# Prompt attention: the offsets of both kv groups of a token tile worked out together

## The chip, the cores and the metric

The kernel runs on one core of one Trainium2 chip. The metric is device time in microseconds (us) of one execution of the whole program; 1792.57 us is the median of three timed runs. The program has five compute engines that run their own instruction queues side by side: TensorE (in the profile PE for its matmuls and PEld for its weight loads), VectorE (DVE), ScalarE (ACT), GpSimd (POOL) and SyncE (SP), the last of which here only starts DMA transfers.

## The reference

One step of a hybrid decoder layer: 1024 prompt tokens and 8 sample tokens (one new token each, with 1024 cached tokens behind it) go through RMS norm, one input projection, native sparse attention (NSA) beside a gated DeltaNet (GDN), one output projection and a SwiGLU feed-forward block. The change touches only the attention of the prompt, which is, per token, head and branch:

```
p_cmp = masked_softmax(q . ck)          # 63 compressed blocks
p_sel = masked_softmax(q . k of the top 16 of 16 blocks)
p_win = masked_softmax(q . kw)          # this token and the 512 before it
out   = gate[0] * p_cmp.cv + gate[1] * p_sel.v + gate[2] * p_win.vw
```

There are 8 heads of 64 values in 2 kv groups of 4 heads. The prompt has 16 blocks of 64 tokens and 16 are selected, so its selected branch is causal attention over everything before the token. Everything is float32; the prompt is `x_prompt` of 1 x 1024 x 1024.

## The kernel before, in words

**Units.** The attention of the prompt is worked in 16 units, a token tile i of 128 tokens and a kv group g of 4 heads, in the order `UNITS = [(i, g) for i in (2,1,0,5,4,3,7,6) for g in range(2)]`, so the two groups of a tile follow each other. A unit goes through five streams.

- *Queries* (`load_queries`, line 990 on): the queries of the unit are fetched, split in a high and a low part, transposed into `qt_a`, and their high half copied into `qo`, whose other rows a GpSimd memset (line 998) has set to zero. Both have three buffers.
- *First pass* (`score_maxima`, line 1014 on): for each branch the scores stand with the 128 tokens on partitions, in a PSUM bank S, of which there are three. Line 1044 multiplies with the high part of the keys, line 1045 with the low part. VectorE takes the negated maximum of a row (line 1049) into `nb`, and ScalarE works out the exponentials with that maximum and adds them up into `sm` (line 1051). A row of over 512 keys is done in two halves. GpSimd memsets (line 1020) fill what a branch leaves empty in `nb` and `sm`.
- *Offsets* (`offset_rows`, line 1056 on): from maximum, sum and gate of each of 3 branches x 4 heads comes one number, the offset -max - ln(sum) + ln(gate), in 18 small VectorE instructions on 128 x 12 values (the logarithm is a polynomial). For i of 4 and more four further instructions join the two halves (lines 1067 to 1072). The high and low parts go to `off`, are transposed on TensorE (line 1105, into a bank S), and VectorE writes them into rows 64 to 112 of `qo` (line 1106).
- *Values* (`values_unit`, line 1111 on): the scores again, now with the keys on partitions, in a bank X (lines 1131 and 1132; the rows of `qo` written by the offsets add the offset to each score), one exponential over 512 values (line 1134, `PF`), a mask for some blocks (line 1137), and the weighted sum of the values in bank O (line 1124).
- *Post* (`write_unit`, line 1151 on): the two halves of O are added, and ScalarE's queue stores the unit in memory (`m_scr`), from where the output projection reads it.

**Order.** The instructions of all streams are written out by `schedule` (line 134). Each stream is a generator; it yields its own estimates of cost and delay in us, or a condition under which it may go on, and `schedule` always takes a stream that is due. The conditions are counters of finished units: Q for queries, A for first passes, F for offsets, C for values, P for posts, W for stores. So

```
yield lambda: "aw" in start and done["Q"] > u and done["F"] >= u - 1
yield lambda: done["A"] > u
yield lambda: done["F"] > u and done["P"] >= u - 0
```

are the conditions of first pass, offsets and values of unit u: a first pass begins once the offsets of the unit before the last are done. A compiler step behind it still moves instructions of an engine by when their operands are expected; tiles with several buffers wait for the reader of the buffer's last content.

**Other work beside it.** Ahead of the attention and in its first part the GDN of the prompt runs. The stream `small_streams` then puts in the work of the samples: their GDN (line 1202 and others) once values of one unit are done (`done["C"] >= 1`), then their attention, for which GpSimd starts 32 indirect DMAs (line 1309) into `gx`, a tile of two buffers that two DMAs of SyncE's queue (`cpx`, `kx`) and a VectorE copy read, then the first two thirds of the output projection (line 1530) as soon as the units they need are stored. The last third (line 1545) comes when all units are stored. The feed-forward block starts behind it.

## Time and profile before

| | |
|---|---|
| median of three timed runs | 1792.57 us (1792.04 to 1793.57) |
| the profiled execution | 1790.07 us |
| its span in the trace | 1788.4 us |
| mean granted clock of TensorE | 0.976 of full speed |
| TensorE matmul, weight loads | 1689.1 us, 1502.5 us busy |
| VectorE, ScalarE, GpSimd | 1123.1 us, 832.6 us, 400.5 us busy |
| prompt attention, first pass to last values | 515.7 to 1034 us of the span |

An engine's busy time is the sum of its instructions; matmuls are pipelined, so a busy TensorE is not one at its peak. The idle time in front of an instruction is put down to what came last of all that it waited for. A granted clock below one is a time in which the chip let TensorE run at the lower of its two speeds (1.2 and 2.4 GHz) for a part. The chain of waits is the sequence of work that ended last, followed back from the end of the program; what stands on it takes time of the whole, what does not stand on it need not.

### The profile page before, as it was taken

What the parts mean: (1) busy time and instruction counts of PE and PEld (TensorE: products, weight loads), DVE (VectorE), ACT (ScalarE), POOL (GpSimd) and SP (SyncE); (2) the same over time, 40 slices, a digit from 0 to 9 for tenths busy, and PEclk for the clock granted to TensorE, in tenths of its full rate; (3) what the DMA queues carried; (4) which work ended last, traced back from release to release, by engine and by line L of the source; (5) the groups of instructions that cost most, each with busy time, mean ns of one, the idle gap of its engine ahead of it and who ended that gap; (6) DMA issues with size and microseconds to landing.
All of it is one profiled execution on the core that took longest, in us unless ns stands there. A gap on an engine that the chain in (4) does not pass through costs nothing.

```text
span 1788.4 us, 32029 instructions
## 1 busy us (share of the span) xinstructions
PE 1689.1 (94%) x11985; PEld 1502.5 (84%) x11985; DVE 1123.1 (63%) x2841; ACT 832.6 (47%) x1986; POOL 400.5 (22%) x405
## 2 busy tenths in 40 slices
PE   7999989989989989989999989999999999999998
PEld 7999989989876465555567769999999999999997
DVE  6458874588468766656754377544444444868786
ACT  5567742222356656646864454433333333633222
POOL 1214330222112221110023453332332334100000
PEclk9999999999989889899999999999999999999999
DMA  7135444665331475552444342233222323533212
GB/s 237 41 103 193 177 157 132 213 214 178 103 103 36 129 211 143 161 158 75 148 117 138 117 134 63 97 102 111 84 84 83 97 82 108 178 126 124 96 59 95
DMA packets 247584, 223.81 MB, mean 125 GB/s; under 512 B 76121, under 2 KB 226145, under 8 KB 245246
## 3 DMA queue, kind: packets, MB, share of 16 engines
q1 hardware_dynamic: 232404, 188.79, 34.2%
q0 software_dynamic: 7152, 22.43, 3.9%
q10 hardware_dynamic: 7874, 10.56, 1.8%
q8 instruction: 94, 1.54, 0.3%
q14 instruction: 60, 0.49, 0.1%
HBM read 149.08 MB, written 60.40 MB: 117 GB/s over the span
## 4 chain that ended last, share of the span: by engine, by line
PE 58%; DVE 4%; DMA 4%; ACT 4%; issue 2%; POOL 1%; SPq 0%; POOLq 0%; ACTq 0%; DVEq 0%
PE X L1763 13%; PE Z L1937 6%; PE V L1763 6%; PE Z L1919 5%; PE O L1124 4%; PE g L1530 4%; PE Y L1763 3%; PE mm L1455 2%; DMA gx<-in_cache_nsa_kv_dram,ix 2%; PE S L1044 2%; PE X L1131 2%; PE S L1045 1%; PE Y L1979 1%; PE X L371 1%; PE X L1132 1%
## 5 line engine op out<-in xcount | busy, mean ns | idle before, releaser
L77 DVE TENSOR_TENSOR q<-q,q 128x256 fp32r<-128x256 f32 (+5 forms) x234 | 139.2, 610 | 50.5 <-ACT q L77 49.0
L77 ACT CAST q<-q 128x256 fp32r<-128x256 f32 (+2 forms) x195 | 90.3, 495 | 129.2 <-DVE q L77 79.2
L1051 ACT ACTIVATE S<-S,nb 128x512 f32<-128x512 f32 (+4 forms) x256 | 119.8, 469 | 47.3 <-DVE nb L1049 39.9
L1049 DVE TENSOR_REDUCE nb<-S 128x1 f32<-128x512 f32 (+4 forms) x154 | 96.2, 636 | 14.7 <-PE S L1045 13.3
L1134 ACT ACTIVATE PF<-X 128x512 f32<-128x512 f32 (+1 forms) x148 | 84.9, 595 | 43.6 <-PE X L1132 38.0
L287 PE MATMUL X<-xh,ch_h 128*128 128x344 f32 x288 | 95.0, 330 | 0.0
L371 PE MATMUL X<-wh,xh 128*128 128x320 f32 (+1 forms) x288 | 93.6, 325 | 0.0
L77 DVE TENSOR_TENSOR q<-q,Y 128x258 f32<-128x258 f32 x40 | 16.9, 424 | 121.4 <-PE Y L1763 85.2
L77 ACT COPY q<-X 128x258 f32<-128x258 f32 x80 | 30.0, 375 | 135.5 <-PE X L1763 135.5
L287 PE MATMUL X<-xl,ch_h 128*128 128x344 f32 x288 | 92.7, 322 | 0.0
L287 PE MATMUL X<-xh,ch_l 128*128 128x344 f32 x288 | 92.7, 323 | 0.0
L371 PE MATMUL X<-wh,xl 128*128 128x320 f32 (+1 forms) x288 | 91.3, 317 | 0.1
L371 PE MATMUL X<-wl,xh 128*128 128x320 f32 (+1 forms) x288 | 91.2, 317 | 0.1
L1722 POOL TENSOR_TENSOR q<-q,q 128x512 f32<-128x512 f32 x40 | 58.8, 1470 | 135.2 <-DVE q L77 107.4
L1497 POOL TENSOR_TENSOR wol<-woraw,woh 128x1024 fp32r<-128x1024 f32 x18 | 43.7, 2434 | 88.5 <-ACT woh L1496 88.5
L1137 DVE TENSOR_TENSOR PF<-PF,keep 128x512 f32<-128x512 f32 (+1 forms) x56 | 40.3, 725 | 30.5 <-ACT PF L1134 30.2
L77 POOL TENSOR_TENSOR q<-q,q 128x258 f32<-128x258 f32 (+1 forms) x44 | 46.5, 1068 | 48.9 <-DVE q L77 48.9
L1124 PE MATMUL O<-PF,vs 128*64 128x512 f32 x144 | 54.5, 647 | 1.5 <-DVE o L1155 1.5
L287 PEld LDWEIGHTS X<-xh,ch_h 128*128 128x128 f32 x288 | 54.9, 191 | 0.2 <-ACT craw L245 0.2
L252 DVE SCALAR_TENSOR_TENSOR cacc<-craw,stt,cacc 128x1024 f32<-128x1024 f32 x36 | 53.1, 1475 | 3.0 <-ACT cacc L250 2.7
L287 PEld LDWEIGHTS X<-xl,ch_h 128*128 128x128 f32 x288 | 54.8, 190 | 0.1
L371 PEld LDWEIGHTS X<-wl,xh 128*128 128x128 f32 x288 | 54.4, 189 | 0.4 <-DVE wl L350 0.4
(758 smaller groups left out, 5582.6 us busy)
## 6 DMA issues: line engine op xcount, KB each, us to landing
q<-in_w_gate_up_dram SPq DMA_DIRECT2D x40, 512.0 KB
woraw<-in_w_out_dram SPq DMA_DIRECT2D x23, 512.0 KB
q<-g_scr SPq DMA_DIRECT2D x22, 516.0 KB
q<-in_w_down_dram SPq DMA_DIRECT2D x22, 512.0 KB
g_scr<-q SPq DMA_DIRECT2D x40, 258.0 KB
k_scr<-pack SPq DMA_DIRECT2D x8, 1280.0 KB
packr<-k_scr SPq DMA_DIRECT2D x8, 1280.0 KB
cpx<-gx SPq DMA_DIRECT2D x64, 128.0 KB
```

The source lines that it names most:

```text
L77: i = op(*args, **kw)
L287: mm(p[:, :CH], lhsT=a[:, k], rhs=b[:, k, CH * c:CH * c + CH], start=k == 0 and j == 0, stop=k == 7 and j == 2)
L371: mm(p[:, :ncol], lhsT=a[:, k, c0:c0 + 128], rhs=b[k][:, :ncol], start=k == 0 and j == 0, stop=k == 7 and j == 2)
L1049: V.tensor_reduce(out=nb[:, y, br, h0:h0 + per], in_=pv, op=OP.max, axis=AX.X, negate=True)
L1051: S.activation(pv[:, h], pv[:, h], AF.Exp, bias=nb[:, y, br, h0 + h:h0 + h + 1], accum_out=sm[:, y, br, h0 + h:h0 + h + 1])
L1124: x = mm(O[64 * (n % 2):64 * (n % 2) + 64], lhsT=v, rhs=pf[:w], start=n < 2, stop=n > last - 2)
L1134: S.activation(pf[:w], p[:w], AF.Exp)
L1530: mm(p[:, :n], lhsT=x[:, k], rhs=y[:, :n], start=i == 0 and j == 0, stop=i == 7 and j == 2)
L1722: plan.setdefault(step, []).append(lambda: eng.tensor_tensor(out, x, y, op=op))
L1763: mm(p, lhsT=w[n][:, x, c], rhs=y[:, k, 258 * q:258 * q + 258], start=new and k == 0 and j == 0, stop=k == nk - 1 and j == 2, skip_group_c ...
L1919: mm(p[:, q], lhsT=w[2 * x + k2][:, y, c], rhs=b[:, k, 258 * q:258 * q + 258], start=k2 == 0 and k == 0 and j == 0, stop=k2 == 1 and k == ...
L1937: mm(p[:, q], lhsT=w[n][:, x, c], rhs=y[:, k, 258 * q:258 * q + 258], start=new and k == 0 and j == 0, stop=k == 1 and j == 2, skip_group_ ...
```

## The change

The offsets are worked out once for the two units of a token tile. `nb` and `sm` become one tile for both groups (128 x 2 x 2 x 3 x 4), allocated by the first; `off` holds both groups; the VectorE instructions have 128 x 24 values where they had 128 x 12 (and 128 x 48 where they had 128 x 24). Two transposes go into one bank S, and two writes follow, one into the `qo` of each unit. The offsets of tile k wait for both first passes (`done["A"] > 2 * k + 1`), and a first pass of tile k may start once the offsets of the tile before the last are done. Queries may be fetched four units ahead of the values, not three, and `qt_a` and `qo` have four buffers. In the changed file lines above 1053 move by two or so, and lines below it by five to seven: 998, 1044, 1045, 1105 and 1106 are now 1000, 1046, 1047, 1111 and 1113, and 1020, 1309, 1530, 1545 are 1022, 1316, 1537, 1552.

```diff
@@ -912,7 +912,7 @@
 
     def attention_queries(start, done):
         for u, (i, g) in enumerate(UNITS):
-            yield lambda: "aq" in start and done["A"] >= u - 1 and done["C"] >= u - 3
+            yield lambda: "aq" in start and done["A"] >= u - 1 and done["C"] >= u - 4
             q = load_queries(start["aq"], g, i)
             yield 0.3, 1.0
             start[u] = q()
@@ -921,15 +921,17 @@
 
     def attention_maxima(start, done):
         for u, (i, g) in enumerate(UNITS):
-            yield lambda: "aw" in start and done["Q"] > u and done["F"] >= u - 1
-            start["n", u] = yield from score_maxima(start["aw"], start["stack", g], start[u], g, i)
+            yield lambda: "aw" in start and done["Q"] > u and done["F"] >= u // 2 * 2 - 2
+            if g == 0:
+                start["n", u // 2] = [start["aw"].tile([128, 2, 2, 3, 4], F32, name=n) for n in ("nb", "sm")]
+            yield from score_maxima(start["stack", g], start[u], g, i, *start["n", u // 2])
             done["A"] += 1
 
     def attention_offsets(start, done):
-        for u, (i, g) in enumerate(UNITS):
-            yield lambda: done["A"] > u
-            yield from offset_rows(start["aw"], *start["n", u], start[u][1], g, i)
-            done["F"] += 1
+        for k in range(len(UNITS) // 2):
+            yield lambda: done["A"] > 2 * k + 1
+            yield from offset_rows(start["aw"], *start["n", k], [start[2 * k + g][1] for g in range(2)], UNITS[2 * k][0])
+            done["F"] += 2
 
     def attention_values(start, done):
         for u, (i, g) in enumerate(UNITS):
@@ -993,8 +995,8 @@
         q2 = aw.tile([128, 4, 2, 64], F32R, name="q2")
         S.mul(q2[:, :, 0], qn, 0.125)
         V.scalar_tensor_tensor(q2[:, :, 1], qn, 0.125, q2[:, :, 0].bitcast(F32), op0=OP.mult, op1=OP.subtract)
-        qt = aw.tile([128, 512], F32R, name="qt_a", bufs=3)
-        qo = aw.tile([128, 512], F32R, name="qo", bufs=3)
+        qt = aw.tile([128, 512], F32R, name="qt_a", bufs=4)
+        qo = aw.tile([128, 512], F32R, name="qo", bufs=4)
         G.memset(qo[64:128].bitcast(F32), 0.0)
 
         def finish():
@@ -1011,11 +1013,11 @@
         w0 = 128 * max(0, i - 4)
         return 128 * (i + 1), w0, 128 * (i + 1) - w0
 
-    def score_maxima(aw, st, q, g, i):
+    def score_maxima(st, q, g, i, nb, sm):
         nk, w0, nw_ = window(i)
         md, mw, mc = maskb[:, 0:128], maskb[:, 128:256], maskb[:, 256 + 64 * i:320 + 64 * i]
         qt, qo = q
-        nb, sm = (aw.tile([128, 2, 3, 4], F32, name=n) for n in ("nb", "sm"))
+        nb, sm = nb[:, :, g], sm[:, :, g]
         for x, v in ((nb, 3e38), (sm, 0.0)):
             G.memset(x[:, 1] if nk <= 512 else x[:, 1, 0], v)
         for br, nm, n, k0 in ((0, "c", 64, 0), (1, "s", nk, 0), (2, "w", nw_, w0)):
@@ -1051,29 +1053,32 @@
                         S.activation(pv[:, h], pv[:, h], AF.Exp, bias=nb[:, y, br, h0 + h:h0 + h + 1],
                                      accum_out=sm[:, y, br, h0 + h:h0 + h + 1])
                     yield 0.43 * per * w / 512.0, 0.3
-        return nb, sm
-
-    def offset_rows(aw, nb, sm, qo, g, i):
+
+    def offset_rows(aw, nb, sm, qos, i):
         yield 0.0, 1.5
-        sh = [128, 12]
-        nb, sms = (x.rearrange("p y b h -> p y (b h)") for x in (nb, sm))
-        off = aw.tile([128, 112], F32R, name="off")
-        G.memset(off[:, 0:64].bitcast(F32), 0.0)
-        ov = off[:, 64:112].rearrange("p (x l) -> p x l", l=4)
+        sh = [128, 24]
+        nb, sms = (x.rearrange("p y g b h -> p y (g b h)") for x in (nb, sm))
+        off = aw.tile([128, 2, 112], F32R, name="off")
+        G.memset(off[:, :, 0:64].bitcast(F32), 0.0)
+        ov = off[:, :, 64:112].rearrange("p g (x l) -> p g x l", l=4)
+
+        def two(x):
+            return x.rearrange("p (g x) -> p g x", g=2)
+
         b, sm = nb[:, 0], sms[:, 0]
         if i >= 4:
             b = aw.tile(sh, F32, name="nbm")
-            d = aw.tile([128, 2, 12], F32, name="nbd")
+            d = aw.tile([128, 2, 24], F32, name="nbd")
             V.tensor_tensor(b, nb[:, 0], nb[:, 1], op=OP.min)
-            V.tensor_tensor(d, b[:, None].to_broadcast([128, 2, 12]), nb, op=OP.subtract)
+            V.tensor_tensor(d, b[:, None].to_broadcast([128, 2, 24]), nb, op=OP.subtract)
             S.activation(d, d, AF.Exp)
             yield 0.0, 0.2
             V.tensor_tensor(sms, sms, d, op=OP.mult)
             V.tensor_tensor(sm, sm, sms[:, 1], op=OP.add)
         elif i == 0:
-            V.tensor_scalar(b[:, 0:4], b[:, 0:4], K[:, GE:GE + 1], None, op0=OP.mult)
-        V.tensor_copy(ov[:, :, 0], b)
-        V.tensor_tensor(ov[:, :, 1], b, ov[:, :, 0].bitcast(F32), op=OP.subtract)
+            V.tensor_scalar(two(b)[:, :, 0:4], two(b)[:, :, 0:4], K[:, GE:GE + 1], None, op0=OP.mult)
+        V.tensor_copy(ov[:, :, :, 0], two(b))
+        V.tensor_tensor(ov[:, :, :, 1], two(b), ov[:, :, :, 0].bitcast(F32), op=OP.subtract)
...
@@ -1094,18 +1099,20 @@
         V.scalar_tensor_tensor(r1, r1, 1.0 / 3, z2, op0=OP.add, op1=OP.mult)
         yield 0.0, 0.2
         V.scalar_tensor_tensor(r1, r1, 1.0, t1, op0=OP.add, op1=OP.mult)
-        V.scalar_tensor_tensor(r1, r1, -2.0, sv['gsc'][:, i, 12 * g:12 * g + 12],
+        V.scalar_tensor_tensor(r1, r1, -2.0, sv['gsc'][:, i],
                                op0=OP.mult, op1=OP.subtract)
         yield 0.0, 0.2
         V.scalar_tensor_tensor(r1, ex, -0.6931471805599453, r1, op0=OP.mult, op1=OP.add)
-        V.tensor_copy(ov[:, :, 2], r1)
-        V.tensor_tensor(ov[:, :, 3], r1, ov[:, :, 2].bitcast(F32), op=OP.subtract)
+        V.tensor_copy(ov[:, :, :, 2], two(r1))
+        V.tensor_tensor(ov[:, :, :, 3], two(r1), ov[:, :, :, 2].bitcast(F32), op=OP.subtract)
         yield 0.0, 0.2
         p = bank("S").bitcast(F32R)
-        tr(p[:112, 0:128], off, identr)
-        V.tensor_tensor(qo[64:112].rearrange("p (h t) -> p h t", h=4),
-                        p[64:112, None, 0:128].bitcast(F32).to_broadcast([48, 4, 128]),
-                        K[64:112, BM:BM + 4, None].to_broadcast([48, 4, 128]), op=OP.mult)
+        for g, qo in enumerate(qos):
+            tr(p[:112, 128 * g:128 * g + 128], off[:, g], identr)
+        for g, qo in enumerate(qos):
+            V.tensor_tensor(qo[64:112].rearrange("p (h t) -> p h t", h=4),
+                            p[64:112, None, 128 * g:128 * g + 128].bitcast(F32).to_broadcast([48, 4, 128]),
+                            K[64:112, BM:BM + 4, None].to_broadcast([48, 4, 128]), op=OP.mult)
         yield 0.1, 1.0
 
     def values_unit(aw, st, q, g, i, keep):
```

(Between its last two pieces stands the polynomial, whose instructions are the same on wider tiles.)

Where the instructions stand now is shown at three places. The first is TensorE's opening of the attention, from the first transposed offsets (`S<-identr,off`) to the first low scores of the values (`X<-qo,kcl`). Before, offsets of the first unit came here, with one and a half first passes above these rows:

```order
L1105 MATMUL S<-identr,off 112x128
L1044 MATMUL S<-kwh,qt_a 128x384
L1045 MATMUL S<-kwl,qo 128x384
L1044 MATMUL S<-kwh,qt_a 128x384
L1045 MATMUL S<-kwl,qo 128x384
L1202 MATMUL g<-sg_S,sg_kz 16x128
L1132 MATMUL X<-qo,kcl 64x512
```

And after, with three first passes above these rows or among them, and matmuls of the samples' GDN (`sg_` names) and of the third unit's queries (`q_6212`) between:

```order
L1233 MATMUL g<-K,sg_vn 128x128 x8
L1111 MATMUL S<-identr,off 112x128 x2
L1046 MATMUL S<-ksh,qt_a 128x256
L1047 MATMUL S<-ksl,qo 128x256
L1046 MATMUL S<-ksh,qt_a 128x256
L1047 MATMUL S<-ksl,qo 128x256
L1005 MATMUL S<-identr,q_6212 128x128 x4
L1139 MATMUL X<-qo,kcl 64x512
```

What moved: the first values stand behind the first passes of a whole tile and about half of the next, and the samples' GDN, which stood behind the first values in part, now stands in front of them.

The second place is GpSimd's queue among the gathers (`gx`). Before:

```order
L1309 DMA gx<-in_cache_nsa_kv_dram,ix 128x1024 x2
L998 MEMSET qo 64x512
L1020 MEMSET nb 128x12
L1020 MEMSET sm 128x12
L1309 DMA gx<-in_cache_nsa_kv_dram,ix 128x1024 x2
L1061 MEMSET off 128x64
L1309 DMA gx<-in_cache_nsa_kv_dram,ix 128x1024 x2
L1020 MEMSET nb 128x12
L1020 MEMSET sm 128x12
L998 MEMSET qo 64x512
L1309 DMA gx<-in_cache_nsa_kv_dram,ix 128x1024 x2
```

And after:

```order
L1022 MEMSET nb 128x12 x2
L1316 DMA gx<-in_cache_nsa_kv_dram,ix 128x1024 x2
L1022 MEMSET sm 128x12 x2
L1316 DMA gx<-in_cache_nsa_kv_dram,ix 128x1024
L1062 MEMSET off 128x2x64
L1316 DMA gx<-in_cache_nsa_kv_dram,ix 128x1024 x6
L1022 MEMSET nb 128x4 x2
L1000 MEMSET qo 64x512
L1022 MEMSET sm 128x4 x2
L1316 DMA gx<-in_cache_nsa_kv_dram,ix 128x1024 x2
L1062 MEMSET off 128x2x64
```

What moved: the memsets of `nb`, `sm` and `off` stand together for two units, and the gathers between them stand in longer rows.

The third place is the end of TensorE's attention, the last weighted values (`O<-PF`) and what stands behind them, down to the last third of the output projection (`mm<-`). Before:

```order
L1131 MATMUL X<-qt_a,kwh 128x512
L1132 MATMUL X<-qo,kwl 128x512
L1124 MATMUL O<-PF,vw 64x512 x5
L1567 MATMUL g<-K,sqo 128x1 x3
L1581 MATMUL Y<-K,rn 128x128 x3
L1545 MATMUL mm<-mh,woh 128x264
```

And after, where the last weighted values stand 24 matmuls of the output projection (line 1537, the former 1530) further up than these:

```order
L1537 MATMUL g<-mh,woh 128x384
L1537 MATMUL g<-ml,woh 128x384
L1537 MATMUL g<-mh,wol 128x384
L1588 MATMUL Y<-K,rn 128x128 x3
L1574 MATMUL g<-K,sqo 128x1 x3
L1588 MATMUL Y<-K,rn 128x128 x3
L1552 MATMUL mm<-mh,woh 128x264 x2
```

What moved: part of the second third of the output projection now stands behind the last values of the attention, where nothing but three small norm sums stood.

## Rows read from the trace of the kernel before

**Rows 1.** The first part of the profile's page: for each engine its busy time in us, the share of the span, and the number of instructions.

```profile
PE 1689.1 (94%) x11985; PEld 1502.5 (84%) x11985; DVE 1123.1 (63%) x2841; ACT 832.6 (47%) x1986; POOL 400.5 (22%) x405
```

**Rows 2.** The table by stretches of the span: from and to, length, busy time of PE, PEld, DVE, ACT and POOL in us (with the number of instructions), the granted clock of TensorE, the busy share of the DMA engines, and GB/s. The first five stretches are the prompt's attention, the last is what follows it.

```profile
510.00:550.00 40.00, 33.62 (x173) 23.68 (x172) 28.47 (x105) 23.34 (x79) 6.89 (x19) 0.83 0.29 81
550.00:604.00 54.00, 52.20 (x281) 32.92 (x280) 45.47 (x153) 35.56 (x125) 8.77 (x22) 0.91 0.23 58
604.00:800.00 196.00, 172.84 (x1044) 110.08 (x1044) 124.05 (x362) 120.03 (x351) 35.74 (x57) 0.94 0.62 174
800.00:930.00 130.00, 122.73 (x731) 76.31 (x728) 86.37 (x245) 95.44 (x273) 9.00 (x15) 0.97 0.33 107
930.00:1034.00 104.00, 99.25 (x474) 73.58 (x473) 40.91 (x60) 44.29 (x72) 44.80 (x22) 0.98 0.42 126
1034.00:1073.00 39.00, 31.82 (x235) 28.98 (x234) 28.36 (x53) 19.92 (x44) 23.43 (x22) 1.00 0.53 143
```

**Rows 3.** The instructions of three lines: the first pass's scores on the compressed keys (its first matmul of each unit), the transposes of the offsets, and the weighted values. After the count: shortest, median and longest duration in ns, then the start of the first and of the last in us.

```profile
L1044 PEld LDWEIGHTS S<-kch,qt_a x64: 186/192/333, 515.7 to 895.9; 128*128 128x128 f32 x64
...
L1105 PE MATMUL S<-identr,off x16: 219/272/356, 542.2 to 927.7; 128*112 128x128 f32 x16
...
L1124 PEld LDWEIGHTS O<-PF,vs x144: 132/136/231, 546.9 to 1026.8; 128*64 128x64 f32 x144
```

**Rows 4.** VectorE's groups by line between 500 and 940 us: out<-in, shapes, count, then busy time in us and mean ns of one, then idle time before them. The lines of the offsets make 25 groups of this list: the write of `qo` (line 1106), and 24 others from the costliest (line 1102) down to line 1072 and, smaller still, the one of the two units with i = 0 (line 1074). Shown are the write, the costliest, and those which tell the two widths 12 and 24 apart.

```profile
L1106 DVE TENSOR_TENSOR qo<-S,K 48x512 fp32r<-48x512 f32 x16 | 11.1, 695 | 8.3 <-PE S L1105 8.0
...
L1102 DVE TENSOR_TENSOR off<-r,off 128x12 fp32r<-128x12 f32 x16 | 3.7, 229 | 0.3
...
L1071 DVE TENSOR_TENSOR sm<-sm,nbd 128x24 f32<-128x24 f32 x8 | 1.4, 181 | 13.6 <-ACT S L1051 11.3 <-ACT nbd L1069 2.3
...
L1068 DVE TENSOR_TENSOR nbd<-nbm,nb 128x24 f32<-128x24 f32 x8 | 1.4, 179 | 0.1
...
L1067 DVE TENSOR_TENSOR nbm<-nb 128x12 f32<-128x12 f32 x8 | 1.4, 169 | 0.3
L1072 DVE TENSOR_TENSOR sm<-sm 128x12 f32<-128x12 f32 x8 | 1.3, 168 | 0.2
```

**Rows 5.** The chain of waits in order of time: start in us, duration in us, what. 82 of its pieces lie on lines 1067 to 1106, 15.3 us together; these are the first and the last of them.

```profile
530.03 0.08 DVE off L1075
...
927.78 0.20 PE S L1105
```

**Rows 6.** The list of waits between 500 and 1040 us: which engine waits at which line, for what, then us in total, how many times, and the longest.

```profile
ACT S L1051 <- DVE nb L1049: 39.9, 43, 4.3
...
PEld S L1044 <- ACT S L1051: 23.1, 34, 1.9
...
PE S L1044 <- ACT S L1051: 6.5, 10, 1.3
```

**Rows 7.** First the instructions of the line of the gathers (columns as in rows 3), with the time from issue to landing of one; then, from the list of waits between 604 and 800 us (columns as in rows 6), GpSimd's memsets.

```profile
L1309 POOL DMA_INDIRECT gx<-in_cache_nsa_kv_dram,ix x32: 933/940/1234, 603.8 to 788.1; - x32
...
DMA to landing us min/median/max: 3.9/4.7/6.5
...
POOL qo L998 <- PE X L1132: 29.5, 5, 13.6
POOL sm L1020 <- DVE t L1087: 23.4, 5, 10.7
...
POOL off L1061 <- PE S L1105: 10.8, 3, 5.4
...
POOL nb L1020 <- ACT S L1051: 7.9, 4, 4.0
...
POOL nb L1020 <- DVE lex L1079: 5.8, 1, 5.8
```

**Rows 8.** The timeline around the last weighted values: start in us, duration, engine, line, what; in brackets the idle time in front of it and what ended that. (ACTq is ScalarE's queue starting a transfer.)

```profile
1025.25 0.33 PE L1530 MATMUL g<-mh,woh 128*128 128x384 f32 x1
...
1025.42 0.33 PE L1530 MATMUL g<-ml,woh 128*128 128x384 f32 x1
...
1033.09 0.19 PEld L1124 LDWEIGHTS O<-PF,vw 128*64 128x64 f32 x2 [2.08 <-DVE PF L1137]
...
1034.20 0.58 ACT L1154 COPY o<-O 64x512 f32<-64x512 f32 x1 [2.75 <-PE O L1124]
...
1035.57 0.68 DVE L1155 TENSOR_TENSOR o<-O,o 64x512 f32<-64x512 f32 x1
...
1036.28 0.58 ACTq L1156 DMA_DIRECT2D m_scr<-o  x1
...
1043.26 0.19 PEld L1545 LDWEIGHTS mm<-ml,woh 128*128 128x128 f32 x1 [1.91 <-DVE ml L153]
```

## The prediction

> **What bounds the kernel now.** I read the page's shares first: TensorE is busy 94% of the span and VectorE 63% [rows 1]. So a faster VectorE pays only where TensorE waits. Next comes the table by stretches [rows 2]. The attention of the prompt runs from about 510 to 1034 us, and the kernel's other stretches hold none of the changed instructions. In those 524 us TensorE is busy 33.62 + 52.20 + 172.84 + 122.73 + 99.25 = 480.6 us, so it is idle for 43.4 us, and 7.2 us more in the 39 us behind it (39 - 31.82). Besides, the granted clock is below one: 0.83, 0.91, 0.94, 0.97, 0.98. A clock of 0.83 over 40 us is 6.8 us of work lost; over the five stretches it is 6.8 + 4.9 + 11.8 + 3.9 + 2.1 = 29.5 us. TensorE's work is the same after the change, matmul for matmul, so all that can be won or lost is part of 43 us of idle time, 30 us of slow clock and 7 us behind the stage.
>
> Where does the change reach that idle time? The chain of waits shows 82 pieces on the lines of the offsets (1067 to 1106), 15.3 us together, between 530 and 928 us [rows 5]. The list of waits shows TensorE's weight loads of the first pass waiting 23.1 us for ScalarE to free a bank S, 34 times, and its matmuls 6.5 us more; ScalarE there waits 39.9 us for VectorE's maxima [rows 6]. GpSimd's list shows its memsets holding up the queue in which the 32 gathers of the samples stand [rows 7].
>
> **The change part by part.**
>
> *Fewer, wider VectorE instructions.* A unit had 19 instructions of offsets, four more in the 8 units with two halves and one more in the 2 units with i = 0: 16 x 19 + 32 + 2 = 338. A pair has 18 and two writes of qo, four more in 4 pairs, one in one: 8 x 20 + 16 + 1 = 177. The write of qo (694 ns) stays at 16 [rows 4]. The others are 24 groups, from 3.7 us down to 1.3 us [rows 4], 59.4 us together, and half of that goes: 29.7 us. They become 24 wide. Rows for both widths stand in the trace: 169 and 168 ns at 12, 179 and 181 ns at 24 [rows 4], 7% more, so 2 us comes back. VectorE loses about 28 us of work. That is no term of the sum; only the next two are.
>
> *The steps on the chain.* 15.3 us of the chain are offset steps [rows 5]. With half as many runs of the same length, 7.7 us leave it at the most, and nothing at the least, if the pass beside them is late next. What is late next is TensorE itself in the stretches where it is 94 to 97% busy, and a bank S in the others. I take -5, two thirds of the way, as the pieces are short and scattered, not one long stall.
>
> *The banks of the first pass.* VectorE works 28.47 + 45.47 + 124.05 + 86.37 + 40.91 = 325 us in the stage [rows 2], and 59 of them are offsets, 18%. If that share of the 29.6 us of bank waits [rows 6] is due to offsets queued ahead of a maximum, it is 5.4 us, and half is 2.7. At the most all of VectorE's relief shows (half of 29.6, 14.8), at the least nothing. I take -2, near the share.
>
> *GpSimd's queue.* Between 604 and 800 us the gathers share it with memsets that wait: sm 23.4, qo 29.5, off 10.8, nb 7.9 and 5.8 us [rows 7], 77 us in all. The 32 gathers start from 603.8 to 788.1 us, 5.9 us apart, and one lands in 4.7 us. The order shows memsets of nb, sm and off in fewer places between the gathers, and the buffers they reset belong to a pair before the last, not to a unit before the last; qo has four buffers for three. So the gathers come sooner, and their transposes too. TensorE is idle for 196 - 172.84 = 23.2 us there. Most of it is not the gathers' alone. A gather's floor, landing and the copies behind it over two buffers, is not far below 5.9 us. I take -3, between 0 and -12 (half the idle time).
>
> *The opening.* The first offsets now need the first pass of both units, so TensorE does the first pass of three units where it did one and a half, before the first weighted values. Before, the first pass starts at 515.7 us, the first offsets are turned at 542.2 and the first values follow at 546.9 [rows 3]; TensorE is idle 6.4 us in 510 to 550 and loses 6.8 us to the clock. The order shows about 20 us of first pass more ahead of the first values. At the rate of that stretch (13.2 us lost in 40) this costs 6.6 us; beside the samples' matmuls that now stand there it may cost nothing. I take +3. From the second pair on, the wait for both units is covered: the values of the pair before are queued beside the first pass of this pair, some 1.4 us of matmul for each block.
>
> *The end.* Before, the last weighted values wait 2.08 us for a mask, TensorE has nothing else, and its output's way through ScalarE, VectorE, memory and back ends with a wait of 1.91 us at 1043.26 [rows 8]. After, 24 matmuls of the output projection stand behind the last values; at 0.17 us from start to start [rows 8] that is 4.1 us of cover. TensorE is idle 7.2 us in 1034 to 1073 [rows 2]. I take -3, between 0 and -7.2.
>
> *The rest.* Eight memsets less on GpSimd, the same transposes, the same DMAs: nothing, since GpSimd is busy 22% of the span [rows 1] and 35.74 of the 196 us with the gathers [rows 2].
>
> Sum: -5 - 2 - 3 + 3 - 3 = -10 us. The profiled execution took 1790.07 us (its span 1788.4 and 1.7 around it), so 1780. The median of the three timed runs is 1792.57, 2.5 above it, so the forecast is 1782.5 us; all times below are on this scale.
>
> **The rivals.**
>
> *A. The relief is hidden.* VectorE is not the bound, the order of TensorE is fixed, and it waits for the next thing instead: the opening's +3 to +6.6 eats the end's -3, and the chain keeps all but a few of its 15.3 us. For it: 34 bank waits of 0.7 us are what three banks cost, with or without offsets. Against it: the offsets are on the chain 82 times. Time 1789 to 1796, say 1792.
>
> *B. The opening decides, and it is slower.* One mechanism: while only first passes run, TensorE goes round the three banks S with short stops, and its clock stays down. In 510 to 550 us it was granted 0.83 of 2.4 GHz, that is, a third of the stretch at 1.2 GHz, with 16% idle [rows 2]. If the 20 us more go at that rate, 6.6 us are lost, and the two following stretches start with the attention behind: the samples' gathers, which wait for the first values before them in the program, start later by as much. Gains of the other terms below 3 us then leave +4 to +10: 1797 to 1803, say 1799. It decides if the first values come later than about 570 us. The Trainium skill, in "TensorE: Matmul & The Clock Gate", section "A second HAM failure mode: psum-queue depth-cycling", says that groups of matmuls cycling through PSUM banks with micro-idles between them make the clock swing between its two levels; by that rule this is the likelier end. The trace agrees with the rule in this stretch: 0.83 here against 1.00 in the 39 us behind the stage, though those have 18% idle.
>
> *C. The gathers were the bound in the middle.* If the freed queue shortens 604 to 800 us by half of its idle time and of its lost clock (23.2 + 11.8, half 17.5, in place of my -3), the sum is -24: 1768. For it: 77 us of waiting memsets in front of gathers [rows 7]. Against it: TensorE did other work for 88% of that time.
>
> *D. It doesn't do what it says.* The instructions are fewer for certain (the order shows it); what could fail is that they run back to back. It falls together with A.
>
> **How the numbers follow.** The forecast's own case (a gain of 4 to 17 us, 1776 to 1789) gets 0.52, C 0.12, A with D 0.20, B 0.16. About 0.2%, 3.6 us, is what a measurement of this kernel can tell from no change: faster means below 1789.0, slower above 1796.2. Faster takes the forecast's case, C and a little of A's lower edge, 0.66; slower takes B without its lower edge, and a little of A's upper one, 0.16; 0.18 is left for no change. The range reaches from the near half of C to the near edge of B, 1770 to 1797.
>
> **What would show it.** Right: VectorE's rows of the offsets at 8 a line and near 180 ns; chain pieces on them near 8 us; bank waits of the first pass below 29 us; the 32 gathers closer than 5.9 us; less than 7.2 us idle in the 39 us behind the last values. Wrong: first values later than 570 us with a clock of 0.83 up to there (B); gathers as far apart as before and a first weighted value as late as before (A). The forecast as a whole is wrong if TensorE's idle time plus lost clock between 510 us and the end of the stage, 73 us now, isn't smaller by 4 us at least.

## The result and the profile after

The changed kernel takes 1810.67 us (median of four runs, 1802.82 to 1814.57) against 1792.3 us for the kernel before on the same chip. The ratio is 1.0101 with a 95% interval of 1.0076 to 1.0125, so the change makes the kernel slower by 18 us. The forecast was 1782.5 us with a range from 1770 to 1797.

The profiled execution is the fastest of the four, 1802.82 us. Its first part of the page and the chain's shares:

```profile
PE 1694.0 (94%) x11985; PEld 1505.7 (84%) x11985; DVE 1106.6 (61%) x2680; ACT 833.8 (46%) x1982; POOL 399.2 (22%) x397
...
PE 55%; DMA 5%; issue 4%; DVE 4%; ACT 4%; POOL 1%; SPq 0%; POOLq 0%; ACTq 0%; DVEq 0%
```

VectorE has 161 instructions and 16.5 us less than in [rows 1], TensorE the same 11985 matmuls. On the chain TensorE has 55% where the page of before has 58%, transfers 5% for 4%, and "issue", time in which an engine waited for nothing that the profile shows, 4% for 2%. These shares are no measure of the loss: up to 516 us the chain now runs along GpSimd's stores of the input projection, with "issue" between them (six pieces of 1.9 to 5.2 us from 490.8 us on), where it ran along TensorE's matmuls.

The table by stretches, to be laid beside [rows 2], and one row each for the whole way from 510 us to the first matmul of the feed-forward block, of after and then, in a fence of its own, of before:

```profile
510.00:550.00 40.00, 30.38 (x174) 22.79 (x172) 21.68 (x69) 18.74 (x61) 12.82 (x25) 0.81 0.34 93
550.00:604.00 54.00, 49.95 (x262) 33.69 (x261) 39.87 (x117) 37.40 (x130) 2.81 (x17) 0.92 0.19 52
604.00:800.00 196.00, 172.68 (x1020) 109.64 (x1020) 118.61 (x319) 118.69 (x352) 36.01 (x55) 0.91 0.58 159
800.00:930.00 130.00, 122.49 (x725) 70.50 (x725) 81.11 (x194) 96.46 (x270) 9.80 (x9) 1.00 0.37 118
930.00:1034.00 104.00, 100.71 (x478) 74.94 (x476) 44.43 (x63) 45.53 (x77) 38.90 (x19) 0.98 0.44 132
1034.00:1073.00 39.00, 31.02 (x189) 26.57 (x187) 21.78 (x41) 15.50 (x28) 16.55 (x12) 0.91 0.50 139
...
510.00:1133.30 623.30, 564.17 (x3304) 394.04 (x3303) 373.84 (x876) 360.05 (x974) 145.19 (x162) 0.95 0.42 123
```

```profile
510.00:1118.90 608.90, 557.32 (x3302) 390.01 (x3301) 389.61 (x1035) 358.13 (x976) 144.21 (x168) 0.95 0.43 125
```

The way to the feed-forward block is 14.4 us longer. TensorE is idle for 59.1 us of it (623.3 - 564.2) where it was 51.6 (608.9 - 557.3). The other 6.9 us are busy time, 564.2 for 557.3 us with the same matmuls. The clock can account for most of that, though over the whole way it is 0.95 in both: counted by stretches as in the prediction, 7.6 + 4.3 + 17.6 + 0 + 2.1 + 3.5 = 35.1 us are lost where it was 29.5 (and nothing in the sixth stretch).

The opening is where it begins. TensorE's timeline of after:

```profile
514.61 0.30 PE L371 MATMUL X<-wh,xl 128*128 128x320 f32 x1
519.97 0.69 PE L1176 MATMUL g<-sg_d,K 8*128 8x64 f32 x2 [5.06 <-DVE sg_d L1174]
520.59 0.69 PE L1185 MATMUL g<-sg_sq,K 128*128 128x64 f32 x2
523.98 0.75 PE L1005 MATMUL S<-identr,q 128*128 128x128 f32 x4 [2.70 <-DVE q L997]
...
525.40 0.42 PE L1046 MATMUL S<-kch,qt_a 128*128 128x64 f32 x1 [0.43 <-ACT qt_a L1006]
```

Behind the last matmul of the input projection (line 371) TensorE stands idle for 5.06 us. Then come two small matmuls of the samples' GDN, then another idle 2.70 us, and only at 523.98 us the transposes of the first queries (line 1005). Before, these followed the projection at once, and the first pass began at 515.7 us [rows 3]; now it begins at 525.40. The line of before:

```profile
514.54 0.46 PE L1003 MATMUL S<-identr,q 128*128 128x128 f32 x4
```

VectorE shows what both waited for:

```profile
518.25 0.48 DVE L393 TENSOR_TENSOR ta<-r,rope 8x320 f32<-8x320 f32 x1 [5.32 <-DMA r<-q]
...
523.50 0.42 DVE L997 SCALAR_TENSOR_TENSOR q<-qn,q 128x256 fp32r<-128x256 f32 x1
```

It waits 5.32 us for a transfer of the samples' own queries (`r<-q`), with the first queries of the prompt (line 997) behind that in its queue. And the queries come late themselves. SyncE's queue of after, then of before:

```profile
514.94 0.37 SPq L1206 DMA_DIRECT2D sg_S<-in_state_gdn_S_dram  x1
515.47 0.86 SPq L994 DMA_DIRECT2D qn<-q_scr  x2
```

```profile
502.74 14.50 SPq L992 DMA_DIRECT2D qn<-q_scr  x5
517.33 5.55 SPq L1199 DMA_DIRECT2D sg_S<-in_state_gdn_S_dram  x8
```

A load of the samples' GDN state (`sg_S`) now stands in front of the first load of queries (`qn`). It waits for the end of the input projection, since its tile lies where the projection's inputs were; the list of waits of SyncE's queue says so:

```profile
SPq L1206 <- PE X L371: 19.3, 1, 19.3
```

So the first queries are fetched at 515.47 us, 12.7 us later than before. The transposes of the offsets and the weighted values, as in [rows 3], and the gathers, as in [rows 7]:

```profile
L1111 PE MATMUL S<-identr,off x16: 225/261/454, 564.4 to 920.1; 128*112 128x128 f32 x16
```

```profile
L1131 PEld LDWEIGHTS O<-PF,vs x144: 132/135/233, 568.2 to 1031.1; 128*64 128x64 f32 x144
```

```profile
L1316 POOL DMA_INDIRECT gx<-in_cache_nsa_kv_dram,ix x32: 932/937/1439, 621.3 to 807.1; - x32
```

First values 21.3 us late, first gather 17.5 us, last gather 19.0 us. The opening by these two points, up to the first values and up to the first gather, of before and then of after:

```profile
510.00:546.90 36.90, 30.52 (x163) 22.63 (x161) 25.85 (x91) 20.47 (x68) 6.68 (x17) 0.81 0.31 84
510.00:603.80 93.80, 85.61 (x452) 56.56 (x451) 73.77 (x257) 58.70 (x203) 15.48 (x40) 0.87 0.26 68
```

```profile
510.00:568.20 58.20, 46.58 (x271) 37.78 (x269) 36.41 (x117) 29.92 (x103) 13.32 (x30) 0.79 0.29 80
510.00:621.30 111.30, 96.05 (x491) 63.64 (x490) 73.63 (x225) 65.48 (x219) 17.34 (x46) 0.89 0.24 65
```

Up to the first gather TensorE is idle for 15.3 us where it was 8.2, so 7.1 of the 7.5 us of new idle time lie in the opening. The lost clock does not: 0.11 x 111.3 and 0.13 x 93.8 are both 12.2 us.

Why should a load change its place in SyncE's queue? The program's list of tiles shows one thing that the diff does not: the fourth buffers of `qt_a` and `qo` make the queries' pool 4096 bytes per partition longer.

```
bytes per partition            before              after
pool of the queries            87776 to 108768     87776 to 112864
  its last buffer of qo        106720 to 108768    110816 to 112864
nat, first of three buffers    111328 to 112736    the same
```

`nat` holds projected rows until they are stored, among them the prompt's queries; in both traces the last of these stores starts at 513 us. The fourth `qo` lies on it. This is theory M: the overlap, and not the pairing, moves the queries behind the samples. Its rival is that the pairing's longer opening does it (theory O). Not only the buffer on `nat` comes late but all that the pool gets first, the mask tile `keep` too (its load starts at 516.5 us, before at 505.6). It goes with its pool the other way as well: in e2 and e9 below `keep` lies in the next pool, which reaches over `nat` in every kernel, and its load starts at 517.4 and 516.4 us. Which rule of the compiler's reordering does that is not seen from here.

### The profile page after: what moved, and what is told of

Same layout as the page of the kernel before. It is cut to its first block, busy times and chain, and to the rows that moved or that the text cites. A ratio compares the mean times of both kernels' runs of the same rounds, so it can differ in the third digit from the quotient of the medians.

```text
span 1801.0 us, 31831 instructions
## 1 busy us (share of the span) xinstructions
PE 1694.0 (94%) x11985; PEld 1505.7 (84%) x11985; DVE 1106.6 (61%) x2680; ACT 833.8 (46%) x1982; POOL 399.2 (22%) x397
## 4 chain that ended last, share of the span: by engine, by line
PE 55%; DMA 5%; issue 4%; DVE 4%; ACT 4%; POOL 1%; SPq 0%; POOLq 0%; ACTq 0%; DVEq 0%
PE X L1770 12%; PE Z L1944 6%; PE V L1770 6%; PE Z L1926 5%; PE O L1131 4%; PE g L1537 3%; PE Y L1770 3%; DMA gx<-in_cache_nsa_kv_dram,ix 3%; PE mm L1462 2%; PE S L1046 2%; ACT S L1053 2%; PE X L1138 2%; PE Y L1986 1%; PE S L1047 1%; PE X L1139 1%
## 5 line engine op out<-in xcount | busy, mean ns | idle before, releaser
L77 ACT CAST q<-q 128x256 fp32r<-128x256 f32 (+2 forms) x195 | 90.3, 494 | 126.2 <-DVE q L77 78.9
L1141 ACT ACTIVATE PF<-X 128x512 f32<-128x512 f32 (+1 forms) x148 | 85.1, 595 | 47.8 <-PE X L1139 45.2
L77 DVE TENSOR_TENSOR q<-q,Y 128x258 f32<-128x258 f32 x40 | 16.9, 424 | 121.0 <-PE Y L1770 87.9
L1144 DVE TENSOR_TENSOR PF<-PF,keep 128x512 f32<-128x512 f32 (+1 forms) x56 | 44.0, 792 | 32.3 <-ACT PF L1141 32.1
L1316 POOL DMA_INDIRECT gx<-in_cache_nsa_kv_dram,ix x32 | 31.3, 979 | 111.9 <-DVE nb L1051 21.0
L371 PEld LDWEIGHTS X<-wh,xl 128*128 128x128 f32 x288 | 55.2, 192 | 0.4 <-DVE xl L153 0.4
```

The costliest lines, as they stand in the source:

```text
L77: i = op(*args, **kw)
L371: mm(p[:, :ncol], lhsT=a[:, k, c0:c0 + 128], rhs=b[k][:, :ncol], start=k == 0 and j == 0, stop=k == 7 and j == 2)
L1141: S.activation(pf[:w], p[:w], AF.Exp)
```

## The experiments

Each ratio is to runs of the kernel before on the same chip: e1 to e4 on one, e5 to e8 on a second, e9 to e12 on a third. Single runs of one kernel differ by up to 13 us here (the kernel before from 1787.5 to 1800.1, e9 from 1788.1 to 1800.9), so the ratios decide and a profile is one draw.

**e1: before, with 4096 unused bytes.**

```diff
+                        pad = aq.tile([128, 1024], F32, name="pad", bufs=1)
+                        V.memset(pad[:, 0:1], 0.0)
```

> The kernel before, with one unused tile of 4096 bytes per partition put into the pool of the queries; nothing else is changed. Theory M (memory): the change's fourth buffers of qt_a and qo make that pool 4096 bytes longer, its end goes from byte 108768 to 112864 and so reaches over the two buffers of nat (from 111328 on), which the last stores of the projected queries still read at 513 us; the first queries then come 12.7 us later, as in the changed kernel (502.74 -> 515.47 us). It expects here the first transposes of the queries at about 524 us and not 514.5, TensorE idle some 5 us in front of them, the first gather about 10 us later than 603.8, and 1798 to 1810 us. Theory O (opening: the wait for the first passes of both units, rival B of the prediction) expects no difference from before: 1790 to 1794 us.

Ratio 1.0069 (1.0047 to 1.0091), median 1806.55 us. The attention's code is as before, and 12 of the 18 us are there. The first gather, at 611.3 us, is 7.5 us late, where about 10 were expected. The same rows of SyncE's queue and of TensorE:

```profile
515.81 0.37 SPq L1201 DMA_DIRECT2D sg_S<-in_state_gdn_S_dram  x1
516.29 0.92 SPq L994 DMA_DIRECT2D qn<-q_scr  x2
```

```profile
521.11 0.69 PE L1171 MATMUL g<-sg_d,K 8*128 8x64 f32 x2 [5.33 <-DVE sg_d L1169]
525.12 0.75 PE L1005 MATMUL S<-identr,q 128*128 128x128 f32 x4 [2.70 <-DVE q L997]
```

The load order of the changed kernel and both its idle times, here 5.33 and 2.70 us, come with 4096 bytes of nothing.

**e8: the same with 2560 bytes**, which end where `nat` begins.

```diff
+                        pad = aq.tile([128, 640], F32, name="pad", bufs=1)
+                        V.memset(pad[:, 0:1], 0.0)
```

> Control of e1: the kernel before with an unused tile of 2560 bytes, so that the queries' pool ends at byte 111328, where nat begins, without reaching over it. Theory M: no difference from before, 1790 to 1795 us, first transposes of the queries at 514 to 517 us. If any shift of the tiles behind it would do what e1 did, it is 1800 us or more.

Ratio 1.0008 (0.9993 to 1.0023). The instructions of all engines stand as before, but for the pad's memset, and the first transposes come at 515.8 us. So it is no shift of tiles that costs; it is reaching over `nat`.

**e2: the change without the overlap.**

```diff
-                        keep = aq.tile([128, CW - KD], BF, name="keep", bufs=1)
+                        keep = aw.tile([128, CW - KD], BF, name="keep", bufs=1)
```

> The changed kernel, with the mask tile keep (2560 bytes) moved from the queries' pool to the next one, so that the queries' pool ends at byte 110304, in front of nat's 111328. All work is the same. Theory M expects the first transposes of the queries back at about 514.5 us, the first values at 552 to 560 us in place of 568.2, the first gather at 603 to 612 us in place of 621.3, and 1786 to 1798 us. Theory O expects the changed kernel's time: 1803 to 1814 us.

Ratio 1.0020 (1.0004 to 1.0035), median 1797.89 us. SyncE's queue has the queries first again, long before the projection ends:

```profile
498.36 20.23 SPq L994 DMA_DIRECT2D qn<-q_scr  x5
518.64 1.53 SPq L1206 DMA_DIRECT2D sg_S<-in_state_gdn_S_dram  x3
```

The first transposes start at 515.7 us and the first values at 560.4, close to what was expected, and the time is at the upper end of its range. The first gather, at 624.1, did not come earlier, against the expectation.

**e12: the changed kernel again**, beside e9 to e11.

> The changed kernel itself, beside the others on one chip. Against e2 it tells what the overlap with nat costs within the change. Theory M: as at first, 1803 to 1814 us, 8 to 15 us more than e2 had over its own before.

Ratio 1.0108 (1.0092 to 1.0123). Against e2 that is 0.88%, 15.8 us, for the overlap alone (uncertain by 0.22%, 4 us; 8 to 15 us were expected).

**e9: the buffers and queries ahead, without the pairing.**

```diff
-            yield lambda: "aq" in start and done["A"] >= u - 1 and done["C"] >= u - 3
+            yield lambda: "aq" in start and done["A"] >= u - 1 and done["C"] >= u - 4
...
-        qt = aw.tile([128, 512], F32R, name="qt_a", bufs=3)
-        qo = aw.tile([128, 512], F32R, name="qo", bufs=3)
+        qt = aw.tile([128, 512], F32R, name="qt_a", bufs=4)
+        qo = aw.tile([128, 512], F32R, name="qo", bufs=4)
```

(and `keep` moved as in e2)

> The kernel before with the fourth buffers of qt_a and qo and the queries up to four units ahead, offsets per unit as before, and keep moved, so that no tile of the queries' pool lies on nat. Together with e3 (the same with the pairing's conditions) it tells what the extra buffers do by themselves. Theory M: without the overlap they are free: 1789 to 1796 us, first gather at 600 to 606 us. If more queries ahead disturb the order of VectorE or ScalarE, 1797 us or more.

Ratio 1.0005 (0.9989 to 1.0021): free to within 4 us, where they overlap nothing. The first gather, at 608.5 us, came later than expected.

**e3: e9 with the pairing's conditions, offsets still narrow.**

```diff
-            yield lambda: "aw" in start and done["Q"] > u and done["F"] >= u - 1
+            yield lambda: "aw" in start and done["Q"] > u and done["F"] >= u // 2 * 2 - 2
...
-            yield lambda: done["A"] > u
+            yield lambda: done["A"] > u // 2 * 2 + 1
```

> As e2 in its buffers and in its conditions (offsets of a tile only when both first passes are done, queries up to four units ahead, keep moved), but with the offsets worked out per unit on 128x12 values as before, one unit after the other. It tells the pairing's order from the wider instructions. If the wider instructions are worth anything (28 us of VectorE's time, the prediction's terms of 5 and 2 us), it is 3 to 8 us slower than e2; if VectorE's relief is hidden (rival A), it is within 2 us of e2.

Ratio 1.0043 (1.0021 to 1.0066). The pairing's conditions, which let the offsets wait for both first passes, cost 0.38% over e9, 7 us (uncertain by 5). The wider instructions (e2 against e3) give 0.23%, 4 us, back, but with these intervals (together 0.27% either way) that is not clear of nothing. So neither "3 to 8 us slower than e2" nor rival A's "within 2 us" is settled by it.

**e4: before, samples started later; e7: before, samples started earlier.**

```diff
-        yield lambda: "free" in start and done["C"] >= 1
+        yield lambda: "free" in start and done["C"] >= 2
```

> The kernel before, with the samples' stream started after the values of two units, not of one. Theory S (the samples' serial stream of GDN, 32 gathers, residual and output projection is what sets the end of the stage): whatever the first gather is late, the end is late by too, some 10 to 15 us: 1800 to 1808 us. Rival: the gathers have slack, TensorE fills the time with the prompt's attention: 1790 to 1795 us.

Ratio 1.0078 (1.0053 to 1.0104), first gather at 632.2 us. As theory S expected. In e7 the condition is `done["A"] >= 1`:

> The kernel before, with the samples' stream started after the first first pass and not after the first values. Counterpart to e4, which started it later (first gather 28 us later, 14 us slower). Theory S: the first gather comes at 590 to 600 us in place of 603.8, and the time is 1784 to 1790 us. If the samples' stream is not what ends last once it is early enough (the prompt's attention is then late next), it stays within 2 us of before.

Ratio 1.0061 (1.0043 to 1.0079), with the first gather 25 us earlier, at 579.0. Theory S falls: the samples' stream is not what the end waits for alone.

**e5: pairs from the second token tile on; e6: e2 with the samples after two first passes; e10: after three.**

```diff
-            yield lambda: done["A"] > 2 * k + 1
-            yield from offset_rows(start["aw"], *start["n", k], [start[2 * k + g][1] for g in range(2)], UNITS[2 * k][0])
-            done["F"] += 2
+            for gs in ((0, 1),) if k else ((0,), (1,)):
+                yield lambda: done["A"] > 2 * k + gs[-1]
...
```

> As e2 (the changed kernel, keep moved, so no overlap with nat), but the offsets of the first token tile are worked out unit by unit; from the second tile on they are worked out for both units together on 128x24 values. TensorE's order then has the first transposed offsets and the first values at their old places in the opening (first values at about 548 us in place of e2's 560.4). Theory S+O (the pairing loses by the late first values, since the samples' stream waits for them): first gather at about 604 us in place of 624.1, and 1786 to 1793 us, 4 to 8 us under e2. Theory P (the pairing loses in every tile, since offsets of two units come as one longer piece in front of the values): no more than 2 us under e2.

Ratio 1.0064 (1.0044 to 1.0084): the first values are back at 547.4 us, but the first gather comes at 616.5, not at 604, and nothing is won. Theory S+O falls. Theory P is met as it was put (not faster than e2), but it does not say why e5 is 0.44% slower than e2. In e6 and e10 the samples' condition of e2 is `done["A"] >= 2` and `done["A"] >= 3`:

> As e2, but the samples' stream starts after two first passes and not after the values of one unit; the pairing is in all tiles. Theory S (the start of the samples' stream sets the end of the stage): first gather 5 to 15 us before e2's 624.1, and 1788 to 1795 us, 3 to 8 us under e2. Theory P: as e2, within 2 us of 1798.

> As e2, but the samples' stream starts after three first passes; e6 started it after two (first gather at 590.6 us, last values 13 us late), e2 after the first values (624.1 us, output projection 9 us late). Theory T (two streams on one TensorE end the stage together: the end comes 85 us behind the last values or 90 us behind the last matmul of the middle part of the output projection, whichever is later): with the first gather between, both are late by less, 1792 to 1798 us. If the pairing itself costs TensorE time wherever the samples stand, 1798 us or more.

Ratios 1.0058 (1.0036 to 1.0080) and 1.0070 (1.0055 to 1.0084), first gathers at 590.6 and 596.0. Theories S and P miss in e6 and theory T in e10, whose other branch, 1798 us or more, is met: earlier samples make the pairing slower.

**e11: pairs in the last two tiles only**, where no gather is left.

```diff
-            for gs in ((0, 1),) if k else ((0,), (1,)):
+            for gs in ((0, 1),) if k >= 6 else ((0,), (1,)):
...
```

> Offsets per unit for the first six token tiles (i = 2, 1, 0, 5, 4, 3), with the conditions of before; together only for the last two (i = 7, 6), behind all gathers. Four buffers, keep moved. Nothing of the samples' stream up to the last gather is disturbed. Theory T expects before's time less what a quarter of the relief is worth: 1789 to 1795 us. A candidate for the best version.

Ratio 1.0032 (1.0019 to 1.0045), 5.7 us slower: a miss, and no better version.

**What the profiles have in common.** One row for each kernel's profiled execution; starts in us of the first values, the first gather, the last weighted values (O), the last matmul of the middle third of the output projection (P) and the feed-forward block's first matmul (F).

| kernel | first values | first gather | O | P | F | F - O | F - P |
|---|---|---|---|---|---|---|---|
| before | 546.9 | 603.8 | 1033.6 | 1028.8 | 1118.9 | **85.3** | **90.1** |
| after | 568.2 | 621.3 | 1039.2 | 1043.8 | 1133.3 | 94.1 | **89.5** |
| e1 | 561.0 | 611.3 | 1040.0 | 1035.2 | 1125.3 | **85.3** | **90.1** |
| e2 | 560.4 | 624.1 | 1033.2 | 1037.8 | 1127.9 | 94.7 | **90.1** |
| e3 | 560.1 | 620.3 | 1032.9 | 1037.5 | 1127.0 | 94.1 | **89.5** |
| e4 | 550.6 | 632.2 | 1036.8 | 1043.5 | 1133.5 | 96.7 | **90.0** |
| e5 | 547.4 | 616.5 | 1033.8 | 1037.4 | 1129.0 | 95.2 | **91.6** |
| e6 | 563.0 | 590.6 | 1046.8 | 1042.0 | 1132.3 | **85.5** | **90.3** |
| e7 | 558.8 | 579.0 | 1044.6 | 1029.6 | 1129.4 | **84.8** | 99.8 |
| e8 | 549.9 | 604.0 | 1036.5 | 1031.7 | 1121.9 | **85.4** | **90.2** |
| e9 | 548.3 | 608.5 | 1042.3 | 1037.4 | 1127.6 | **85.3** | **90.2** |
| e10 | 557.3 | 596.0 | 1044.1 | 1039.3 | 1129.7 | **85.6** | **90.4** |
| e11 | 547.2 | 608.8 | 1034.9 | 1034.2 | 1122.8 | 87.9 | **88.6** |
| e12 | 569.4 | 622.6 | 1046.4 | 1051.0 | 1140.4 | 94.0 | **89.4** |

A single profile scatters: e8 has the instructions of before and e12 those of after, and their F stand 3.0 and 7.1 us later. What holds in all fourteen is the two last columns: the feed-forward block starts some 85 us behind the last values or 90 us behind the projection, whichever is later, to within 1.5 us; from its start to the end of the span it is 667.7 to 670.1 us. The two numbers can be told apart only where one stream is late alone, 84.8 in e7 and 89.4 to 90.1 in after, e2, e3, e4 and e12. By these both bounds bind at the same moment before: 1033.6 + 84.8 = 1118.4, 1028.8 + 90.1 = 1118.9. The two streams share one TensorE, and either one put ahead makes the other late: after, e2, e3, e4, e5 and e12 are late by P, e7 by O, e1, e6, e8, e9 and e10 by both, as before, with P always some 4.8 us in front of O, and e11 stands between. That is theory T. As a forecast of times it failed in e10 and e11. It says which stream is late in each kernel; it does not say why a pair's wait makes the sum of both worse, and no run here does.

## Why the prediction was wrong

*The opening.* This is the step that failed. It was put at +3 us, at most +6.6, for first passes in a stretch of slow clock, with the samples' matmuls as cover, and "the same DMAs" were put at nothing. The order rows showed those matmuls moved forward, and the prediction took them for cover, without asking what they wait for. They wait for a transfer, and so does VectorE. The DMAs are the same, but the first load of queries had moved behind a load on SyncE's queue that must wait for the input projection; that queue's order shows it, and the prediction did not look there, nor had it a term for the fourth buffers that moved it. Measured: 5.06 + 2.70 us of idle TensorE, the first values 21.3 us late where e2, the same change without the overlap, has them 13.5 us late, and 12 us (e1) to 16 us (e12 against e2) at the end.

*The clock.* The prediction looked for it in the opening, where it had no part: 12.2 us lost up to the first gather, as before. Behind it some 5 us more are lost in all: more in 604 to 800 (0.91 for 0.94) and 1034 to 1073 (0.91 for 1.00), less in 800 to 930 (1.00 for 0.97) [rows 2]. No term had that. It is not the draw of one profile alone: e12's five executions have a mean granted clock of 0.970, the 23 of before beside them 0.974, which is, as an estimate, 7 of their 19 us. Whether the new order lowers the clock there or the waits do, no run shows.

*"TensorE's work is the same, so all that can be lost is part of the idle time"* was no bound for the loss: new idle time can be made, and was. The prediction's last sign says so: idle time and lost clock from 510 to 1034 us, 73 us before, are 47.8 + 31.6 = 79 us after.

*Fewer, wider instructions.* Right. All groups of the offsets but the write of `qo` sum to 30.5 us, where they took 59.9 (the 59.4 of the prediction leave out the one for i = 0); 28 us less was forecast. VectorE's busy time as a whole fell by 16.5 us only: part of these short instructions overlap their neighbours in the trace, and the other instructions take 6.3 us more (1069.9 to 1076.2). Three of the rows:

```profile
L1113 DVE TENSOR_TENSOR qo<-S,K 48x512 fp32r<-48x512 f32 x16 | 10.6, 691 | 4.2 <-PE S L1111 4.0
...
L1107 DVE TENSOR_TENSOR off<-r,off 128x24 fp32r<-128x24 f32 x8 | 1.6, 203 | 0.2
L1101 DVE SCALAR_TENSOR_TENSOR r<-r,t 128x24 f32<-128x24 f32 x8 | 1.4, 181 | 0.2
```

*The steps on the chain (-5).* They did leave it: 53 pieces and 10.4 us, where there were 82 and 15.3 [rows 5]. But the way is longer all the same: on the chain between 495 us and the feed-forward block the gathers have 47 us where they had 36. ("Issue" has 45 where it had 28, but 18 of these lie in front of 516 us, beside the input projection.) What leaves a chain is no gain while another wait stands ready.

*The banks (-2).* Nothing came. The waits of [rows 6] after the change:

```profile
ACT S L1053 <- DVE nb L1051: 39.0, 42, 3.6
...
PEld S L1046 <- ACT S L1053: 23.1, 36, 1.6
...
PE S L1046 <- ACT S L1053: 8.2, 17, 0.8
```

39.0, 23.1 and 8.2 us for 39.9, 23.1 and 6.5. Offsets in VectorE's queue were not what held up the maxima; this part of rival A was right.

*GpSimd's queue (-3).* Nothing came, and rival C falls with it. The memsets that waited between the first and the last gather did wait less, 43 us in all, where they had 77 [rows 7]; these are the longest of each tile after the change, in 621 to 808 us:

```profile
POOL nb L1022 <- ACT S L1053: 17.2, 1, 17.2
...
POOL qo L1000 <- PE X L1139: 12.3, 4, 5.4
...
POOL off L1062 <- PE S L1111: 6.9, 1, 6.9
...
POOL sm L1022 <- DVE t L1092: 3.7, 2, 2.3
```

But from the first to the last gather it is 185.8 us, before 184.3, and 182 to 195 in all fourteen kernels: neither waiting memsets nor the pairing set their pace.

*The end (-3).* The cover came: after the last values at 1039.2 us matmuls of the output projection go on to 1043.8. But behind them the norm's small sums now wait uncovered:

```profile
1048.01 0.83 PE L1574 MATMUL g<-K,sqo 128*128 128x1 f32 x6 [3.17 <-DVE sqo L1569]
...
1051.48 1.62 PE L1588 MATMUL Y<-K,rn 128*128 128x128 f32 x6 [2.65 <-DVE rn L1579]
```

The wait moved from the last values to the projection, 3.17 + 2.65 us, since that is now what ends last (P in the table).

*The rivals.* B gave the direction, and first values at 568.2 us are just short of its mark of 570, but that was luck: 15.8 us of the loss are the overlap's, which B does not name, and its price of 4 to 10 us was half of the 18 at the most. Its mechanism, a clock held down by more first passes, is not what made it. Up to the first values the clock is indeed low for longer (0.79 over 58.2 us, 0.81 over 36.9 before), but e1, with no first pass more, has 0.77 over 51.0 us, and up to the first gather no more is lost than before. The rule that B cited from the Trainium skill ("TensorE: Matmul & The Clock Gate", "A second HAM failure mode: psum-queue depth-cycling"), of a clock that swings while matmuls cycle through PSUM banks, is neither shown nor refuted by that. Without the overlap, e2's 1.0020, 3.6 us above before's, lies at the upper edge of rival A. Whether VectorE's relief is hidden, or worth some 4 us and outweighed by the wait for both groups, e2 and e3 do not separate.

Put together from the ratios: buffers +0.9 us (e9), waiting for both groups +6.8 (e3 against e9, uncertain by 5), wider instructions -4.1 (e2 against e3, uncertain by 4.9), overlap +15.8 (e12 against e2, uncertain by 4). The first three sum to +3.6 us and all four to +19.4, which is e2 and e12 again: each is a difference to the run before it, so the sums prove nothing of their own.

## What to carry to other kernels

A buffer more is not free because there is room for it: it moves the end of its pool, and where that end reached over a tile that was still read, loads that stood early in a queue came behind others. So compare where the pools lie before and after, and read the order of the DMA queues as well as that of the engine that bounds. And where a tuned order has two streams end at the same moment, moving either against the other cost (0.6 to 0.8% in e4 and e7), while halving the work of the offsets, on an engine that was not the bound, gave no more than the wait for it cost.

## What was not expected of the hardware

The scatter of the changed kernel is a scatter of the clock: its four executions had spans of 1801.0, 1805.2, 1812.6 and 1812.8 us at mean granted clocks of 0.974, 0.973, 0.969 and 0.969. Of the 11.8 us between the first and the last, 0.005 x 1801 = 9 us are the clock, with the same instructions in the same order.
